# The convolution's taps of two recurrences, moved from VectorE, ScalarE and GpSimd to TensorE

## The chip, the cores and the metric

The kernel runs on one core of a Trainium2 chip. The metric is the device time of one launch in microseconds (us); lower is better. The core has a matrix engine (TensorE, in the profile PE, with its weight loads apart as PEld), a vector engine (VectorE, DVE), a scalar engine (ScalarE, ACT), a general engine (GpSimd, POOL) and a queue that issues transfers (SyncE, SP). Each engine executes its own instruction list in order and waits for others by semaphores.

## The reference

Two layers work on two token streams, `x` and `ctx` (256 tokens of 1024 features each). In each layer a token's 1024 modulated features go through `w_in`; the first 1024 columns of the product feed a convolution path and the rest a linear recurrence (RWKV) of 8 heads. The two halves, 512 features each, are joined and multiplied by `w_out`; then comes a gated feed-forward block.

The convolution path is what the change touches:

```
def conformer_conv(u, conv_w, conv_b, cnorm_g, cnorm_b):
    val, gate = jnp.split(u, 2, axis=-1)
    z = val * jax.nn.sigmoid(gate)
    z = dwconv(z, conv_w) + conv_b          # 31 taps along the 256 tokens, one filter per channel
    z = group_norm(z, CONV_GROUPS, cnorm_g, cnorm_b, LN_EPS)   # 8 groups of 64 channels
    return jax.nn.silu(z)
```

The depthwise convolution has 31 taps, 512 channels and 256 tokens. The scale and shift of every norm ("modulation") come from a vector `c` times `ada_w` (1024 x 6144 per layer), cut into six parts.

## The kernel before

Activations are kept with features on the partitions: a 512-feature tensor is four tiles of 128 x 256 ("four features" below). Weights arrive as 512 KB tiles of 128 x 1024 fp32 through `raw` (L345 to L349), which has four slots in turn. A large weight is split into a high and a low part, `wh` (ScalarE, L341) and `wl` (VectorE, L342; a few on GpSimd, L365), and multiplied as three fast products (`mm3`). The modulation weights are not split: `ada_steps` (L478) multiplies each tile with a 32-column vector in two fp32 products of 512 columns, and after eight tiles the sum goes through ScalarE (tile `T2b`), four small products with `sel` and a VectorE addition.

A recurrence (`rwkv`, L766) works in chunks: products of the input projection (`w_in`), the inverse of small triangular matrices by some hundred dependent VectorE steps (L953 to L969) with 32x32 and 64x64 products, `reads` (L1035), `values` (L1052 to L1071), and then a `chain` of four steps for each of two head groups (L1083 to L1133). Four recurrences are in the program. The first (stream `ctx`, layer 0, about 100 to 260 us) and the last (stream `x`, layer 1, about 1100 to 1350 us) run in the mode "wide": both groups side by side, and with a filler. The filler is a generator of other work, of which the loop over the chain draws six steps (`fill(FILL)`) after each of its eight chain steps: first the convolution's input projection (`conv_in`, four steps), then the modulation vectors (`ada_steps`, 16 steps). After the recurrence of these two the convolution `conv` is emitted whole.

The order in the code is not the order of an engine. A scheduler takes all instructions, with the emitted order as priority, and gives each engine a fixed list by its own estimate of when operands and buffers are ready. So taps emitted after the recurrence are placed into gaps of VectorE, ScalarE and GpSimd during it.

The taps before: of the 30 taps beside the middle one, VectorE takes 13 (first recurrence) or 14 (last) as multiply-add in place (L726), ScalarE 3 or 4 as a product (L730), GpSimd 14 or 12 as a product (L732); GpSimd adds those of ScalarE and its own (L733). The tile `tap` has two buffers, shared by ScalarE and GpSimd. VectorE joins the two sums and the bias at L737. Then comes the group norm (L745): a mean product with a constant, a subtraction on VectorE, a square on ScalarE, a sum product, a reciprocal square root, and four products that spread it. A third convolution, of `z` in layer 0, is done by GpSimd alone, five taps at a time in the background of a feed-forward block and a recurrence. In PSUM the filler's lane has the tag `pb` (two buffers) to itself while the recurrence has the others.

Of the kernel before, what the change touches and what calls it, by code (L numbers as in the profile page):

```python
# [11 lines left out]
AF = mybir.ActivationFunctionType  # L12
ALU = mybir.AluOpType

P = 128
D = 1024
NF = 8
T = 256
# [6 lines left out]
LN_EPS = 1e-5  # L25
# [12 lines left out]
NPOOL, NPOOLE, NPOOLC = (14, 3), (12, 4), (30, 0)  # L38
NTAP = 2

# [127 lines left out]
def _layout(a):  # L168
    f = {}
    n = {k: np.asarray(v) for k, v in a.items()}  # L170
# [38 lines left out]
    for l in range(2):  # L209
        f[f"ada{l}"] = n["ada_w"][l].reshape(4, 2, P, 12, 512).transpose(3, 0, 2, 1, 4).reshape(48, P, 1024)  # L210
        w = n["w_in"][l]
# [7 lines left out]
        f[f"wo{l}"] = (n["w_out"][l].reshape(NF, P, D))  # L219
        lo = np.zeros((P, 2, 1024), np.float32)  # L220
# [15 lines left out]
        w = n["w_in_2"][l]  # L236
# [22 lines left out]
class Prog:  # L259
# [441 lines left out]
    def conv(self, l, z, acc, npool, hold=False):  # L701


        nc = self.nc
        o = COLS[f"convw{l}"][0]
        taps = sorted((j for j in range(31) if j != 15), key=lambda j: abs(j - 15))
        nv, na = 30 - npool[0] - npool[1], npool[1]
        parts = [("v", taps[:nv]), ("a", taps[nv : nv + na]), ("p", taps[nv + na :])]

        order = []  # L710
        for k, js in parts:
            order += [((i + 0.5) / len(js), k, j) for i, j in enumerate(js)]
        order.sort()
        zc = [acc[:, f, :] for f in range(4)]
        for f in range(4):
            w = lambda j: self.cols[:, o + 4 * j + f : o + 4 * j + f + 1]
            av = self.T1([P, T]) if nv else None
            if nv:
                nc.vector.tensor_scalar(av, z[:, f, :], w(15), None, ALU.mult)
                nc.gpsimd.memset(zc[f], 0.0)  # L720
            else:
                nc.gpsimd.tensor_scalar(zc[f], z[:, f, :], w(15), None, ALU.mult)
            for i, (_, k, j) in enumerate(order):
                d, s = slice(max(0, 15 - j), min(T, T + 15 - j)), slice(max(0, j - 15), min(T, T + j - 15))
                if k == "v":
                    nc.vector.scalar_tensor_tensor(av[:, d], z[:, f, s], w(j), av[:, d], ALU.mult, ALU.add)  # L726
                else:
                    t = self.t(self.pool, [P, T], "tap", bufs=NTAP)
                    if k == "a":
                        nc.scalar.mul(t[:, d], z[:, f, s], w(j))  # L730
                    else:
                        nc.gpsimd.tensor_scalar(t[:, d], z[:, f, s], w(j), None, ALU.mult)  # L732
                    nc.gpsimd.tensor_add(zc[f][:, d], zc[f][:, d], t[:, d])  # L733
                if i % 5 == 4:
                    yield
            if nv:
                nc.vector.scalar_tensor_tensor(zc[f], av, self.col(f"convb{l}", f), zc[f], ALU.add, ALU.add)  # L737
            else:
                nc.gpsimd.tensor_scalar(zc[f], zc[f], self.col(f"convb{l}", f), None, ALU.add)
            yield  # L740
        while hold and not self.go:
            yield
        self.group_norm(zc, f"cng{l}", f"cnb{l}", LN_EPS, AF.Silu)
# [668 lines left out]
    def first(self):  # L1412
        nc = self.nc
# [4 lines left out]
        alone = {"r": ("ps", "acc00", "acc01"), "t": ("acc10", "acc11"), "b": ("pb",), "c": ("acc11",), "cs": ("acc10",)}  # L1418
# [6 lines left out]
        def wide(l, x, s0, ada, perm, before=None):  # L1425

            def filler():

                steps = itertools.chain(self.conv_in(l, x, fl(self.x[0])), self.ada_steps(l, ada))
# [14 lines left out]
            self.on("c")  # L1444
            drain(self.conv(l, fl(self.x[0]), fl(self.x[1]), (NPOOL, NPOOLE)[l]))
# [37 lines left out]
        self.bg = self.conv(0, zx, acc, NPOOLC, True)  # L1483
# [155 lines left out]
```

## Time and profile before

| what | us |
|---|---|
| time, median of 3 runs (lowest, highest) | 2779.92 (2776.57, 2785.88) |
| the profiled execution's own time | 2783.58 |
| its span, first to last instruction | 2781.8 |
| busy in the span: PE | 2632.1 (95%) |
| busy: PEld | 2291.3 (82%) |
| busy: DVE | 1716.4 (62%) |
| busy: ACT | 1327.3 (48%) |
| busy: POOL | 670.2 (24%) |

The profile is of one execution. Busy time is the time in which an engine had an instruction in work, and a busy TensorE can be at either of two clocks, so its share has to be read with the granted clock beside it (1.00 is 2.4 GHz, 0.50 is 1.2 GHz). A matmul in fp32 leaves two records in the trace, so a row "x4" of fp32 products may be two products. Idle time is put down to the engine or transfer that ended it.

### The profile page before, as it was taken

What the parts mean: (1) busy time and instruction counts of PE and PEld (TensorE: products, weight loads), DVE (VectorE), ACT (ScalarE), POOL (GpSimd) and SP (SyncE); (2) the same over time, 40 slices, a digit from 0 to 9 for tenths busy, and PEclk for the clock granted to TensorE, in tenths of its full rate; (3) what the DMA queues carried; (4) which work ended last, traced back from release to release, by engine and by line L of the source; (5) the groups of instructions that cost most, each with busy time, mean ns of one, the idle gap of its engine ahead of it and who ended that gap; (6) DMA issues with size and microseconds to landing.
All of it is one profiled execution on the core that took longest, in us unless ns stands there. A gap on an engine that the chain in (4) does not pass through costs nothing.

```text
span 2781.8 us, 53780 instructions
## 1 busy us (share of the span) xinstructions
PE 2632.1 (95%) x22398; PEld 2291.3 (82%) x22398; DVE 1716.4 (62%) x2703; ACT 1327.3 (48%) x2015; POOL 670.2 (24%) x669
## 2 busy tenths in 40 slices
PE   7889989999889998899899899999999999999998
PEld 4866867888678896866699899889899898889897
DVE  3885778645577555984555655666655655755655
ACT  5523654434565346433544544654544544644543
POOL 0388999920130001384200000010000000100000
PEclk9989989999899999979899999999999999999999
DMA  7345425334323354234355555524555555425653
GB/s 250 109 145 175 147 84 180 132 130 157 117 77 116 136 182 144 95 137 153 117 187 185 194 183 188 193 87 156 182 187 185 182 188 174 166 83 182 205 184 120
DMA packets 118768, 430.71 MB, mean 155 GB/s; under 512 B 13174, under 2 KB 13686, under 8 KB 118524
## 3 DMA queue, kind: packets, MB, share of 16 engines
q1 hardware_dynamic: 118524, 427.28, 45.2%
q8 instruction: 175, 2.87, 0.4%
q14 instruction: 69, 0.57, 0.1%
HBM read 425.13 MB, written 2.10 MB: 154 GB/s over the span
## 4 chain that ended last, share of the span: by engine, by line
PE 78%; DVE 11%; ACT 4%; POOL 3%; issue 2%; DMA 2%; SPq 0%; ACTq 0%; DVEq 0%; POOLq 0%
PE pb L333 33%; PE acc L333 25%; PE ps L333 19%; DVE wl L342 3%; DVE T1c L726 1%; POOL tap L732 1%; DVE S L964 1%; DVE T L962 1%; DMA raw<-in_ada 1%; DVE x L621 1%; ACT wh L341 1%; POOL x L733 1%; PE acc L438 1%; DMA raw<-in_wr 0%; DVE T2b L620 0%
## 5 line engine op out<-in xcount | busy, mean ns | idle before, releaser
L342 DVE TENSOR_TENSOR wl<-raw,wh 128x1024 fp32r<-128x1024 f32 (+1 forms) x654 | 811.9, 1245 | 622.2 <-ACT wh L341 391.7
L341 ACT CAST wh<-raw 128x1024 fp32r<-128x1024 f32 (+1 forms) x654 | 681.9, 1046 | 892.3 <-PE pb L333 345.8
L333 PE MATMUL pb<-xf,wh 128*128 128x256 f32 (+1 forms) x2560 | 486.4, 289 | 12.6 <-ACT T1b L585 4.1
L333 PE MATMUL pb<-S,wh 128*128 128x256 f32 x2560 | 492.0, 289 | 4.8 <-DVE S L631 1.8
L333 PEld LDWEIGHTS pb<-xf,wh 128*128 128x128 f32 (+1 forms) x2560 | 409.8, 194 | 26.7 <-DVE T1b L588 6.6
L333 PEld LDWEIGHTS pb<-S,wh 128*128 128x128 f32 x2560 | 408.5, 192 | 22.4 <-issue 11.8
L333 PE MATMUL ps<-S,wh 128*128 128x256 f32 x2048 | 390.4, 287 | 0.6 <-ACT S L460 0.5
L333 PE MATMUL pb<-xf,wl 128*128 128x256 f32 (+1 forms) x1280 | 371.2, 291 | 8.7 <-DVE wl L342 8.7
L365 POOL TENSOR_TENSOR wl<-raw,wh 128x1024 fp32r<-128x1024 f32 x22 | 54.9, 2504 | 1340.4 <-ACT wh L364 826.9
L333 PE MATMUL pb<-S,wl 128*128 128x256 f32 x1280 | 367.4, 287 | 2.0 <-DVE wl L342 2.0
L333 PEld LDWEIGHTS ps<-S,wh 128*128 128x128 f32 x2048 | 326.8, 192 | 9.0 <-issue 3.4
L333 PE MATMUL ps<-S,wl 128*128 128x256 f32 x1024 | 293.4, 286 | 0.6 <-DVE wl L342 0.6
L333 PEld LDWEIGHTS pb<-xf,wl 128*128 128x128 f32 (+1 forms) x1280 | 248.1, 194 | 16.7 <-DVE wl L342 11.5
L333 PEld LDWEIGHTS pb<-S,wl 128*128 128x128 f32 x1280 | 245.4, 192 | 6.6 <-issue 3.0
L333 PE MATMUL acc<-wh,T 128*128 128x512 f32 x704 | 206.3, 393 | 0.0
L333 PEld LDWEIGHTS ps<-S,wl 128*128 128x128 f32 x1024 | 196.7, 192 | 2.8 <-issue 1.4
L333 PE MATMUL acc<-wh,T1b 128*128 128x512 f32 x528 | 157.5, 396 | 3.5 <-ACT T1b L341 3.5
L732 POOL TENSOR_SCALAR tap<-z,cols 128x255 f32<-128x255 f32 (+14 forms) x120 | 149.2, 1252 | 0.0
L333 PEld LDWEIGHTS acc<-wh,T 128*128 128x128 f32 x704 | 126.9, 189 | 23.6
L732 POOL TENSOR_SCALAR tap<-x,cols 128x246 f32<-128x246 f32 (+6 forms) x104 | 111.4, 1079 | 46.1 <-DVE x L671 46.0
L733 POOL TENSOR_TENSOR x<-x,tap 128x247 f32<-128x247 f32 (+8 forms) x132 | 106.8, 809 | 34.4 <-ACT tap L730 28.0
L733 POOL TENSOR_TENSOR z<-z,tap 128x255 f32<-128x255 f32 (+14 forms) x120 | 112.8, 940 | 3.9
(445 smaller groups left out, 3968.7 us busy)
## 6 DMA issues: line engine op xcount, KB each, us to landing
raw<-in_fu SPq DMA_DIRECT2D x132, 512.0 KB, 3.2
raw<-in_ada SPq DMA_DIRECT2D x96, 512.0 KB, 4.3
raw<-in_pu SPq DMA_DIRECT2D x88, 512.0 KB, 4.2
raw<-in_qu SPq DMA_DIRECT2D x88, 512.0 KB, 3.7
raw<-in_fd SPq DMA_DIRECT2D x66, 512.0 KB, 3.2
raw<-in_wr SPq DMA_DIRECT2D x51, 512.0 KB, 3.6
raw<-in_pd SPq DMA_DIRECT2D x44, 512.0 KB, 4.1
raw<-in_qd SPq DMA_DIRECT2D x44, 512.0 KB, 3.8
```

What stands on the lines that cost most here:

```text
L333: return self.nc.tensor.matmul(out, lhsT, rhs, start=start, stop=stop, **kw)
L341: self.nc.scalar.copy(hi, src)
L342: self.nc.vector.tensor_sub(lo, src, hi.bitcast(F32))
L365: self.nc.gpsimd.tensor_sub(lo, r, hi.bitcast(F32))
L438: nc.tensor.transpose(pt[f // 2][:, f % 2, b, :], yb[b][:, f * P : f * P + P], self.cst("ident"))
L621: nc.vector.tensor_add(x[b][:, s], x[b][:, s], t)
L726: nc.vector.scalar_tensor_tensor(av[:, d], z[:, f, s], w(j), av[:, d], ALU.mult, ALU.add)
L732: nc.gpsimd.tensor_scalar(t[:, d], z[:, f, s], w(j), None, ALU.mult)
L733: nc.gpsimd.tensor_add(zc[f][:, d], zc[f][:, d], t[:, d])
L962: nc.vector.tensor_mul(tv, tj[:, k + 1 : 32, k : k + 1].broadcast_to([P, m, k + 1]), X[:, k : k + 1, 0 : k + 1].broadcast_to([P, m, k + 1]))
L964: nc.vector.tensor_sub(X[:, k + 1 : 32, 0 : k + 1], X[:, k + 1 : 32, 0 : k + 1], tv)
```

## The change

In the first and in the last recurrence the taps become TensorE products. For each of the four features the 31 taps are 31 fp32 products of a 128x128 diagonal matrix (the filter's weights of one tap on the diagonal) with a shifted slice of `z`, summed in one PSUM tile; ScalarE adds the bias on the way out. The diagonals are loaded from a new input `cd`, 16 tiles of 512 KB per layer with eight taps each, through the same four `raw` slots. The new generator `conv_pe` and its group norm are steps of the filler, between `conv_in` and `ada_steps`. The third convolution keeps its GpSimd form; `conv` loses the code for the other engines.

```diff
+TAPS = sorted(range(31), key=lambda j: abs(j - 15))
...
+        cw = n["conv_w"][l].reshape(31, 4, P)
+        cd = np.zeros((4, 4, P, 8, P), np.float32)
+        for i, j in enumerate(TAPS):
+            for f_ in range(4):
+                cd[f_, i // 8, np.arange(P), i % 8, np.arange(P)] = cw[j, f_]
+        f[f"cd{l}"] = cd.reshape(16, P, D)
...
+    def conv_pe(self, l, z, acc):
+
+        for f in range(4):
+            pc = self.ps((P, T))
+            for i, j in enumerate(TAPS):
+                if i % 8 == 0:
+                    r = self.raw(f"cd{l}", f * 4 + i // 8)
+                d, s = slice(max(0, 15 - j), min(T, T + 15 - j)), slice(max(0, j - 15), min(T, T + j - 15))
+                self.mm(pc[:, d], r[:, i % 8 * P : i % 8 * P + P], z[:, f, s], i == 0, i == 30)
+                if i % 8 == 7:
+                    yield
+            self.nc.scalar.activation(acc[:, f, :], pc, AF.Identity, bias=self.col(f"convb{l}", f))
+            yield
+        self.group_norm([acc[:, f, :] for f in range(4)], f"cng{l}", f"cnb{l}", LN_EPS, AF.Silu)
+        yield
...
-        alone = {"r": ("ps", "acc00", "acc01"), "t": ("acc10", "acc11"), "b": ("pb",), "c": ("acc11",), "cs": ("acc10",)}
+        alone = {"r": ("ps", "acc00", "acc01"), "t": ("acc10", "acc11"), "b": ("pb",), "cs": ("pb",)}
...
-                steps = itertools.chain(self.conv_in(l, x, fl(self.x[0])), self.ada_steps(l, ada))
+                steps = itertools.chain(self.conv_in(l, x, fl(self.x[0])), self.conv_pe(l, fl(self.x[0]), fl(self.x[1])),
+                                        self.ada_steps(l, ada))
...
-            self.on("c")
-            drain(self.conv(l, fl(self.x[0]), fl(self.x[1]), (NPOOL, NPOOLE)[l]))
```

In the rows below, `raw` with `csil` is a modulation product, `raw` with `x_67` a tap (`x_67` is the convolution's input of that recurrence, `x_68` its result), `acc` and `ps` are PSUM tiles of the recurrence and `pb` one of the filler. First PE's list in the first recurrence before, after the last product of `conv_in` and one modulation half:

```order
L1035 MATMUL acc_239_1489<-const,S_496 128x128 x4
L333 MATMUL pb_2215<-raw_2216,csil 32x512 x2
L1035 MATMUL acc_240_1495<-const,S_496 128x128 x4
L333 MATMUL pb_2215<-raw_2220,csil 32x512 x2
L1052 MATMUL acc_244_1504<-const,S_299 64x128 x4
L333 MATMUL pb_2215<-raw_2224,csil 32x512 x2
L333 MATMUL acc_245_1511<-S_885,S_493 64x64 x4
L333 MATMUL acc_246_1512<-S_885,S_493 64x64 x4
L333 MATMUL pb_2215<-raw_2228,csil 32x512 x2
```

The 32 modulation tiles of this recurrence stand in this way between its rows. After the change, where `conv_in` ends and the first such tiles stood, PE's list reads:

```order
L341 MATMUL pb_2105<-xf_242,wl_2102 128x256
L341 MATMUL pb_2157<-x_67,raw_2158 128x256
L341 MATMUL pb_2157<-x_67,raw_2158 128x255 x2
L341 MATMUL acc_236_1468<-S_1098,S_496 64x64 x2
L341 MATMUL acc_237_1469<-S_1098,S_496 64x64 x2
```

The taps have taken the places of the modulation tiles. Those have moved behind the chain; PE's list after, towards the end of the same recurrence:

```order
L341 MATMUL pb_2635<-raw_2644,csil 32x512 x2
L341 MATMUL pb_2635<-raw_2648,csil 32x512 x2
L341 MATMUL pb_2654<-const,T2b_2652 128x2 x4
L341 MATMUL pb_2660<-raw_2661,csil 32x512 x2
L341 MATMUL pb_2660<-raw_2665,csil 32x512 x2
L341 MATMUL pb_2660<-raw_2723,csil 32x512 x2
L341 MATMUL pb_2660<-raw_2727,csil 32x512 x2
L341 MATMUL pb_2733<-const,T2b_2731 128x2 x4
```

Nothing of the recurrence stands between these rows any more. The group norm's products of the convolution (`x_68`, `T1b`) now stand among the chain's, in PE's list after:

```order
L341 MATMUL ps_2834<-S_956,st_2572 64x64 x3
L341 MATMUL pb_2490<-T1b_2487,const 128x256
L341 MATMUL pb_2494<-T1b_2487,const 128x256
L341 MATMUL acc_446_2810<-T_445_2808,S_1785 64x64
L341 MATMUL acc_447_2811<-T_445_2808,S_1785 64x64
```

A product of the norm that has to wait holds up the chain's products behind it. On POOL the list after goes from the recurrence's set-up to the third convolution:

```order
L470 TENSOR_TENSOR S_2952<-T1b_2993,S_2950 128x256
L939 TENSOR_TENSOR S_1867<-S_1867,T_501_3043 128x256
L939 TENSOR_TENSOR S_1867<-S_1867,T_504_3055 128x256
L732 TENSOR_SCALAR z_5712<-z_3103,cols 128x256
L736 TENSOR_SCALAR tap_5747<-z_3103,cols 128x255
```

Before, the 124 instructions of the recurrence's own taps (on `x_67` and `x_68`) stood ahead of the `z` rows.

## Rows read from the trace of the kernel before

**Rows 1.** the page's chain that ended last, by engine and by line

```profile
PE 78%; DVE 11%; ACT 4%; POOL 3%; issue 2%; DMA 2%; SPq 0%; ACTq 0%; DVEq 0%; POOLq 0%
PE pb L333 33%; PE acc L333 25%; PE ps L333 19%; DVE wl L342 3%; DVE T1c L726 1%; POOL tap L732 1%; DVE S L964 1%; DVE T L962 1%; DMA raw<-in_ada 1%; DVE x L621 1%; ACT wh L341 1%; POOL x L733 1%; PE acc L438 1%; DMA raw<-in_wr 0%; DVE T2b L620 0%
```

**Rows 2.** windows: length, busy us (instructions) by engine, PEclk, DMA share, GB/s

```profile
163.42:258.05 94.63, 94.10 (x1262) 61.83 (x1262) 60.31 (x131) 33.58 (x62) 71.15 (x82) 0.82 0.53 183
1199.35:1350.00 150.65, 145.92 (x1559) 101.01 (x1560) 93.68 (x200) 53.06 (x93) 81.55 (x97) 0.84 0.40 141
130.00:163.42 33.42, 25.99 (x333) 22.42 (x331) 33.42 (x60) 9.12 (x16) 31.07 (x30) 1.00 0.35 117
1150.00:1199.35 49.35, 40.61 (x495) 35.87 (x495) 48.11 (x94) 17.37 (x28) 30.77 (x31) 0.98 0.34 118
```

**Rows 3.** waits of PE in 130 to 163 us: us in total, times, longest

```profile
PE pb L333 <- DVE wl L342: 3.8, 3, 1.9
PE acc L333 <- DVE S L1029: 2.7, 2, 2.4
```

**Rows 4.** windows, VectorE's taps (L726) alone

```profile
131.00:189.00 58.00, 24.48 (x39) 0.91 0.50 170
1168.00:1224.00 56.00, 24.86 (x42) 0.94 0.51 179
```

**Rows 5.** windows of 10 us in both wide recurrences

```profile
190.00:200.00 10.00, 10.00 (x174) 7.46 (x169) 5.30 (x9) 5.88 (x9) 9.68 (x12) 0.70 0.26 92
...
200.00:210.00 10.00, 10.00 (x151) 8.69 (x149) 3.44 (x8) 3.33 (x6) 6.89 (x10) 0.50 0.01 4
...
230.00:240.00 10.00, 10.00 (x156) 6.79 (x153) 3.49 (x10) 2.18 (x5) 7.35 (x10) 1.00 0.76 278
...
1245.00:1255.00 10.00, 10.00 (x124) 7.74 (x125) 3.51 (x7) 2.17 (x4) 9.52 (x13) 0.50 0.01 2
```

**Rows 6.** timeline of PE: start, duration, instruction, count, idle time before it

```profile
56.51 1.02 PE L333 MATMUL ps<-wa,S 128*128 128x256 f32 x4
57.37 2.05 PE L333 MATMUL acc<-S,T 128*128 128x512 f32 x4
```

**Rows 7.** timeline, PE weight loads of 128x128 fp32

```profile
30.29 0.97 PEld L333 LDWEIGHTS ps<-const,T 128*128 128x128 f32 x8
```

**Rows 8.** timeline, PE, products with split weights

```profile
48.18 0.40 PE L333 MATMUL ps<-xf,wh 128*128 128x256 f32 x2
48.42 0.28 PE L333 MATMUL ps<-xf,wl 128*128 128x256 f32 x1
48.54 0.40 PE L333 MATMUL acc<-xf,wh 128*128 128x256 f32 x2
```

**Rows 9.** timeline, PE, modulation tiles with nothing else beside them

```profile
23.20 1.05 PE L333 MATMUL acc<-raw,csil 128*32 128x512 f32 x4
...
28.92 1.05 PE L333 MATMUL pb<-raw,csil 128*32 128x512 f32 x4 [0.21 <-DMA raw<-in_ada]
```

**Rows 10.** windows, the same modulation stage

```profile
20.00:30.00 10.00, 7.80 (x37) 1.93 (x34) 0.56 (x3) 1.63 (x3) 0.00 (x0) 1.00 0.91 318
```

**Rows 11.** timeline, ACT and PE, at the end of the last recurrence's chain

```profile
1270.32 0.50 ACT L730 ACTIVATE tap<-x,cols 128x247 f32<-128x247 f32 x1 [3.59 <-POOL x L733]
...
1270.85 0.38 ACT L1102 ACTIVATE xf<-acc 64x256 f32<-64x256 f32 x1
...
1271.28 0.69 PE L333 MATMUL acc<-xf,S 128*64 128x64 f32 x16 [1.56 <-ACT xf L1102]
...
1277.11 0.26 PE L333 MATMUL ps<-zer 1*128 1x256 bf16 x1 [1.40 <-ACT S L1131]
```

**Rows 12.** timeline, POOL and PE, in the second recurrence

```profile
390.49 2.58 POOL L365 TENSOR_TENSOR wl<-raw,wh 128x1024 fp32r<-128x1024 f32 x1
...
400.00 0.74 PE L333 MATMUL ps<-S,S 64*32 64x32 f32 x28 [4.16 <-DVE S L850]
```

**Rows 13.** windows, the same place

```profile
390.00:400.00 10.00, 2.98 (x14) 2.42 (x12) 5.47 (x7) 6.99 (x12) 10.00 (x7) 0.59 0.33 107
```

More of the change, by code (lines that the diff above doesn't have):

```diff
@@ L36 @@
 NLAST = 2, 4
-NPOOL, NPOOLE, NPOOLC = (14, 3), (12, 4), (30, 0)
 NTAP = 2
+TAPS = sorted(range(31), key=lambda j: abs(j - 15))
 QB, QE, QC, EVERY = (2, 3, 4, 5), (2, 3, 4, 5), (1,), 2
@@ L699, in mixed_in, with conv @@
         return mix
-    def conv(self, l, z, acc, npool, hold=False):
+    def conv_pe(self, l, z, acc):
[12 more added lines that the diff above has]
+        yield
+    def conv(self, l, z, acc):
         nc = self.nc
         o = COLS[f"convw{l}"][0]
[L706 to L713, printed above, removed]
         zc = [acc[:, f, :] for f in range(4)]
@@ L716, in conv @@
             w = lambda j: self.cols[:, o + 4 * j + f : o + 4 * j + f + 1]
[L717 to L723, printed above, removed]
-                d, s = slice(max(0, 15 - j), min(T, T + 15 - j)), slice(max(0, j - 15), min(T, T + j - 15))
[L725 to L733, printed above, removed]
+            nc.gpsimd.tensor_scalar(zc[f], z[:, f, :], w(15), None, ALU.mult)
+            for i, j in enumerate(TAPS[1:]):
+                d, s = slice(max(0, 15 - j), min(T, T + 15 - j)), slice(max(0, j - 15), min(T, T + j - 15))
+                t = self.t(self.pool, [P, T], "tap", bufs=NTAP)
+                nc.gpsimd.tensor_scalar(t[:, d], z[:, f, s], w(j), None, ALU.mult)
+                nc.gpsimd.tensor_add(zc[f][:, d], zc[f][:, d], t[:, d])
                 if i % 5 == 4:
                     yield
[L736 to L739, printed above, removed]
+            nc.gpsimd.tensor_scalar(zc[f], zc[f], self.col(f"convb{l}", f), None, ALU.add)
             yield
-        while hold and not self.go:
+        while not self.go:
             yield
@@ L1482, in first @@
         self.go = False
-        self.bg = self.conv(0, zx, acc, NPOOLC, True)
+        self.bg = self.conv(0, zx, acc)
         self.mods, self.every = self.ada_steps(1, QC), EVERY
```

## The prediction

> **What bounds the kernel now.** I read the chain of waits first: 78% of it is PE, in products of all kinds, 11% VectorE, and of the taps only 1% on VectorE and 2% on GpSimd [rows 1]. So what a change does to TensorE's own work is what counts, and elsewhere only where PE stands still. Next I read the two wide recurrences in windows [rows 2]. Each has two parts. In the first part (130 to 163 us, 1150 to 1199 us) VectorE is full (33.42 of 33.42 us, 48.11 of 49.35) and PE has gaps: 7.4 us (33.42 - 25.99) and 8.7 us (49.35 - 40.61). The waits name VectorE as what ends the gaps, by its weight splits and the evacuations L1029 [rows 3], and of VectorE's time there and just after it the taps take 24.5 and 24.9 us [rows 4]. In the second part (163 to 258, 1199 to 1350 us) PE is busy for 94.10 of 94.63 us and 145.92 of 150.65 us, but at a mean granted clock of 0.82 and 0.84 [rows 2]. In 10 us slices the clock stands at full speed (1.00, 2.4 GHz) while modulation tiles stream in (DMA share 0.76 at 230 us), and at half speed (0.50, 1.2 GHz) where only small products run and hardly a byte arrives (DMA share 0.01 at 200 and at 1245 us) [rows 5]. So half speed is where the recurrence has TensorE to itself, with many short products of 64 columns.
>
> **What is added to TensorE.** 31 taps for four features are 124 fp32 products in a recurrence, 248 in all, of a 128x128 diagonal with at most 256 columns. The nearest row is a product of the same type, stationary size and columns: four records, two products, begin at 56.51 and the next row begins at 57.37, so a product takes 0.43 us [rows 6]. Taps off the middle are shorter: by 2 x (1 + ... + 15) = 240 columns in a feature, so the mean is 256 - 240/31 = 248.3 columns, 0.417 us. 124 x 0.417 = 51.7 us, and twice that is **+103.4 us** on the engine that ends the chain. The order of the changed kernel has them in PE's list between the recurrence's products, in the places where the modulation products stood; those are not removed, they come later.
>
> Here the Trainium skill speaks against the change more strongly than the row. "TensorE: Matmul & The Clock Gate", Part 3 ("The mechanism"), says that a weight load runs beside a product in flight only where the two use different row groups of the array; a 128-row diagonal after another 128-row diagonal uses the same. By that rule every load would stand by itself. The two products of [rows 6] also have full 128-row stationaries that differ, and they follow at 0.43 us; the trace does not agree here, and I take the row.
>
> **What is given back.** (1) The gaps of PE in the first parts: with some 25 us of VectorE's work gone from each, VectorE is ahead, and what is late next is PE, which has the taps to fill the gaps with. 7.4 + 8.7 = **-16.1 us**. (2) Gaps of the second parts, 0.5 and 4.7 us, partly behind ScalarE and its taps (a tap at 1270.32 to 1270.82 stands just ahead of the copy that PE waits 1.56 us for [rows 11]): **-4 us**. (3) The clock. If full speed were held through both second parts, PE's busy time would shrink by 94.10 x 0.18 = 16.9 and 145.92 x 0.16 = 23.3 us, 40.2 in all; that is one end. The other is nothing, since the modulation tiles that kept the clock up at 230 us leave their place, and in the last recurrence the changed list still has a stretch of some 300 small products without one tap. I take 60%, **-24 us**, nearer to the full end because the taps stand in most of the stretches that ran at half speed and are dense products, like those of the slices at 1.00.
>
> **What is lost in other places.** (4) The modulation products. Their 32 tiles stood between the recurrence's rows, hidden behind its products; now most of them follow one another at the end, with y's norm alone between them, and behind them 16 transposes of the next input. Where nothing stood beside them, at the start of the kernel, four tiles took 28.92 - 23.20 = 5.72 us, with PE waiting for the transfer [rows 9] and a DMA share of 0.91 [rows 10]: 1.43 us a tile, against 1.05 of PE's work. 32 x (1.43 - 1.05) = 12.2 us in a recurrence, 24.3 us in both, is one end, nothing the other. Four slots are loaded ahead and a part of the tiles still stands beside the chain, but a half also ends in a chain of ScalarE, PE and VectorE (`T2b`), so I take **+10 us**, the lower side of the middle. The 32 new transfers of 512 KB cost nothing as long as they hide behind taps: a tile feeds 8 x 0.417 = 3.3 us of products and arrives alone in 1.43 us. (5) The group norm. It was outside the chain; now its 12 products wait in PE's list among the chain's products, each for VectorE or ScalarE, and what waits behind one is the chain itself, which VectorE and ScalarE in turn wait for. The chain's own waits of that kind are 1.56 and 1.40 us [rows 11]. Twelve of them, in two recurrences half hidden, would be 12 x 1.4 = 16.8 us; the other end is nothing, where the operands are ready before PE gets there. I take **+8 us**. (6) GpSimd. Without some 250 tap instructions it reaches the third convolution sooner, and so the weight splits that wait in its list: one began at 390.49 us, PE stood still for 4.16 us until 400.00 [rows 12] and was busy for 2.98 of the 10 us there [rows 13]. I take **-6 us**, between 0 and the 7.0 us of that gap. ScalarE loses 28 taps and gains 8 evacuations, beside TensorE: nothing.
>
> **The sum.** 103.4 - 16.1 - 4 - 24 + 10 + 8 - 6 = +71.3 us. On the profiled execution's 2783.58 that is 2854.9; the median of the runs is 3.7 below that execution, so **2851 us**, 2.6% slower.
>
> **Rivals.**
> A. *All that can be given back is given back*: the clock in full (-40.2), all gaps (-16.1 and -5.2), GpSimd (-7), no new wait: 103.4 - 68.5 = +35, 2815 us. For it: the taps are the kind of dense work at which the clock stood at 1.00. Against it: the stretch without taps has nothing to raise its clock, and the norm's products are in the chain's way in the list.
> B. *The end of the recurrence binds*: modulation tiles at the speed of their transfers (+24.3), the norm in full (+16.8), and the clock gives back a third (-13): 103.4 - 16.1 - 4 - 13 + 24.3 + 16.8 - 6 = +105, 2885 us. For it: the tiles stand one behind the other in the list, with nothing of the recurrence between them.
> C. *Weight loads are not hidden.* 248 products are 496 records, each with its load of 0.121 us (0.97 us for eight [rows 7]): +60 us on the sum, 2911 us. This is what the page's rule would give. Against it stands the 0.43 us of [rows 6].
> D. *Faster: a tap takes one pass.* If a diagonal product ran like those of the split weights, three of 256 columns in 0.36 us (48.18 to 48.54 [rows 8]), 0.12 us each, the taps would cost 248 x 0.12 = 30 us, less than the 56 us that the gaps and the clock have room for (16.1 and 40.2), and would fit into them: 30 - 16.1 - 4 - 40.2 + 10 + 8 - 6 = -18, 2762 us. It decides from a tap of 0.19 us downward, where 248 taps cost the 48 us that the other terms then give. Against it: the split tiles are cast to another type first and `cd` is not, and the modulation tiles, fp32 straight from `raw` as well, run at fp32 speed.
> E. *The change doesn't do what it says*: the list has all 124 taps in each recurrence and none on VectorE, so this has no share.
>
> **How the numbers follow.** Forecast 0.74 (own range 2821 to 2881: half the distance between the ends is 20 us for the clock, 12 for the modulation tiles, 8 for the norm and 6 for gaps and GpSimd, as independent ones together 26, and 4 more for the price of a product), A 0.10, B 0.09, C 0.03, D 0.04. A change below 0.3% (about 8 us) can't be told from none. D has half its chance below that bound and half within it, and all other cases are slower: faster 0.02, within 0.02, slower 0.96. The range of 8 in 10 takes the forecast's own and A's: 2813 to 2883 us.
>
> **What would show it.** A run of taps in the timeline at 0.43 us a product bears out the sum's first term; 0.12 would be D, 0.67 (0.43 and two loads of 0.121) C. PE's gaps between 130 and 163 us and the VectorE waits in them should be gone. The granted clock of the small products should be above 0.9 in the first recurrence, and still show a slice at half speed in the last one. Behind the chain, modulation tiles should be spaced by 1.0 to 1.4 us, and waits of PE for a transfer of `in_ada` should appear. Waits for `T1b` or `x_68` inside the chain bear out (5). The forecast is wrong if the two recurrences together grow by less than 35 or by more than 105 us.

## The result and the profile after

The changed kernel takes 2879.57 us (median of 4 runs, 2875.63 to 2883.16), the kernel before beside it 2782.90 us (4 runs). The ratio is 1.0348, 95% interval 1.0328 to 1.0368: 3.5% slower. Forecast were 2851 us, slower, and a range of 2813 to 2883 us. So the sign and the range held, and the size was short by some 25 us: +97 us against +71.

The page of the changed kernel, the chain that ended last, by engine and by line (compare [rows 1]):

```profile
PE 83%; DVE 8%; ACT 4%; DMA 3%; issue 1%; POOL 1%; SPq 0%; ACTq 0%; DVEq 0%; POOLq 0%
PE pb L341 38%; PE acc L341 25%; PE ps L341 19%; DVE wl L350 2%; DMA raw<-in_ada 2%; DVE x L629 1%; ACT wh L349 1%; PE acc L446 0%; DVE S L965 0%; ACT L392 0%; DMA raw<-in_wr 0%; DVE S L852 0%; DVE T L963 0%; DVE T2b L628 0%; POOL tap L736 0%
```

The taps of VectorE and GpSimd have left the chain, PE's share rose from 78% to 83%, and loads of `in_ada` went from 1% to 2%. Next the changed kernel in stretches, as windows (us, busy us and instructions by engine, PEclk, DMA share, GB/s): the first parts, the half-speed stretches and the ends of the two recurrences.

```profile
134.00:163.00 29.00, 29.00 (x319) 27.24 (x320) 22.95 (x57) 7.52 (x12) 0.00 (x0) 1.00 0.32 110
1200.00:1240.00 40.00, 40.00 (x489) 37.55 (x487) 36.70 (x92) 13.53 (x21) 0.00 (x0) 1.00 0.36 120
170.00:200.00 30.00, 30.00 (x387) 24.70 (x384) 10.29 (x19) 10.73 (x16) 1.90 (x2) 0.72 0.11 37
1250.00:1290.00 40.00, 38.95 (x501) 33.08 (x496) 13.44 (x26) 12.62 (x20) 1.90 (x2) 0.57 0.09 28
260.00:330.00 70.00, 59.19 (x417) 28.53 (x414) 23.09 (x52) 22.16 (x43) 1.61 (x2) 0.87 0.76 270
1350.00:1420.00 70.00, 61.50 (x371) 26.93 (x369) 20.42 (x53) 16.75 (x32) 7.70 (x12) 0.83 0.64 226
```

In the first parts PE has no gap left (29.00 of 29.00, 40.00 of 40.00; before 7.4 and 8.7 us [rows 2]). The half-speed stretches are still there. New are the ends: PE stands still for 10.8 and 8.5 us in 70, and its clock is not full there either. In the kernel before the stretches behind the chain read:

```profile
258.00:337.60 79.60, 77.80 (x574) 66.64 (x570) 55.35 (x88) 45.90 (x70) 77.00 (x78) 1.00 0.39 127
1300.00:1336.10 36.10, 34.42 (x143) 21.19 (x140) 18.87 (x41) 15.38 (x27) 7.66 (x10) 0.86 0.04 12
```

To see where the 97 us are, I cut each profile at five marks that all kernels have: the first load of `wc`, the first `T1b` from `pb` of the feed-forward block, the first subtraction in the third convolution's norm, the last load of `wr`, the first load of `pu`. The second mark (421 us in the kernel before) lies inside the second recurrence, so the stage "first rec." holds the beginning of that one too. Stage lengths, in us over the kernel before:

| kernel | start | first rec. | second | third | last rec. | rest |
|---|---|---|---|---|---|---|
| before (length) | 92.4 | 328.9 | 324.3 | 378.6 | 418.4 | 1239.2 |
| changed | +4.0 | +52.3 | -6.5 | -4.0 | +48.6 | +1.1 |
| changed, again | +0.4 | +54.3 | -6.5 | -3.9 | +48.4 | +0.9 |
| changed, middle tap alone | +2.6 | +0.2 | +0.3 | -1.3 | +1.0 | -1.6 |
| before, middle tap alone | +2.8 | -7.1 | -3.1 | +0.8 | -10.8 | +4.6 |
| changed in the first alone | +2.2 | +52.5 | -6.6 | -4.1 | +13.6 | -1.6 |
| changed in the last alone | +5.5 | -3.9 | -0.4 | +0.2 | +37.2 | -2.3 |
| changed, bank counter kept | +2.9 | +53.0 | -1.3 | +5.4 | +43.7 | +5.2 |

And what the clock took: over windows of 10 us, the sum of PE's busy time x (1 - granted clock), called "loss" below, from the first load of `wc` to the first of `wo`, and from the last load of `wr` to the last of `wo`. It is read from one profile each; the changed kernel's two profiles give 47.2 and 49.5 us. It measures where the clock was low; it is not time one to one, as a run below shows.

| kernel | loss, first | loss, last | together | PE idle, together |
|---|---|---|---|---|
| before | 21.1 | 23.9 | 45.0 | 32.9 |
| changed | 20.3 | 26.9 | 47.2 | 30.6 |
| changed, middle tap alone | 27.0 | 40.0 | 67.0 | 21.5 |
| before, middle tap alone | 21.2 | 21.6 | 42.8 | 19.7 |
| before, modulation late | 37.3 | 27.0 | 64.3 | 49.6 |
| changed, modulation first | 17.6 | 28.3 | 45.9 | 18.0 |
| changed, taps and modulation in turn | 17.4 | 20.0 | 37.4 | 20.4 |
| changed, taps among the small products | 20.1 | 9.5 | 29.6 | 23.5 |
| changed, again | 21.6 | 27.9 | 49.5 | 31.5 |
| changed in the first alone | 21.5 | 31.1 | 52.6 | 38.6 |
| changed in the last alone | 17.9 | 19.7 | 37.6 | 27.0 |
| changed, bank counter kept | 27.9 | 19.7 | 47.6 | 28.9 |

The loss did not fall from 45 to 21, as the forecast had it; it stayed.

### The profile page after: what moved, and what is told of

It is laid out like the page before. It is cut to its first block, busy times and chain, and to the rows that moved or that the text cites. A ratio compares the mean times of both kernels' runs of the same rounds, so it can differ in the third digit from the quotient of the medians.

```text
span 2877.3 us, 54424 instructions
## 1 busy us (share of the span) xinstructions
PE 2731.5 (95%) x22894; PEld 2376.7 (83%) x22894; DVE 1635.5 (57%) x2579; ACT 1311.4 (46%) x1990; POOL 450.9 (16%) x425
## 3 DMA queue, kind: packets, MB, share of 16 engines
q1 hardware_dynamic: 123132, 444.06, 44.6%
## 4 chain that ended last, share of the span: by engine, by line
PE 83%; DVE 8%; ACT 4%; DMA 3%; issue 1%; POOL 1%; SPq 0%; ACTq 0%; DVEq 0%; POOLq 0%
PE pb L341 38%; PE acc L341 25%; PE ps L341 19%; DVE wl L350 2%; DMA raw<-in_ada 2%; DVE x L629 1%; ACT wh L349 1%; PE acc L446 0%; DVE S L965 0%; ACT L392 0%; DMA raw<-in_wr 0%; DVE S L852 0%; DVE T L963 0%; DVE T2b L628 0%; POOL tap L736 0%
## 5 line engine op out<-in xcount | busy, mean ns | idle before, releaser
L341 PEld LDWEIGHTS ps<-S,wh 128*128 128x128 f32 x2048 | 327.5, 192 | 10.8 <-issue 4.2
L736 POOL TENSOR_SCALAR tap<-z,cols 128x255 f32<-128x255 f32 (+14 forms) x120 | 143.3, 1203 | 0.0
L341 PE MATMUL pb<-x,raw 128*128 128x254 f32 (+15 forms) x496 | 115.7, 389 | 0.0
L341 PE MATMUL acc<-wl,T 128*128 128x512 f32 x352 | 113.1, 395 | 0.0
```

Of the source, the lines that this page charges most:

```text
L341: return self.nc.tensor.matmul(out, lhsT, rhs, start=start, stop=stop, **kw)
```

## The experiments

Theory: a tap costs TensorE its full 0.42 us, wherever it stands; what the other engines' taps had cost before comes back, but the new order spends as much. Rivals: the order alone makes the difference; the weight loads do; the clock was to come back and something stopped it.

**The changed kernel with the middle tap alone.**

```diff
-            for i, j in enumerate(TAPS):
+            for i, j in enumerate(TAPS[:1]):
...
+            for _ in range(3):      # as many filler steps as with all taps
+                yield
```

> The changed kernel with the middle tap alone: 240 of the 248 tap products are left out (and 24 of 32 loads of diagonals). Theory 1 (0.417 us a tap, nothing hidden): 240 x 0.417 = 100 us less than the changed kernel, 2780 us. Theory 2 (each tap also waits for its weight loads, 0.67 us): 160 us less, 2720 us. Theory 3 (a part of the taps stands in gaps or speeds up the clock): clearly less than 100 us are saved, about 2800 us or more.

Measured: 2779.31 us, ratio 0.9989 (0.9969 to 1.0009). Against the changed kernel's 1.0348 that is 0.0359 x 2783 = 99.9 us for 240 taps, 0.416 us each, the number of Theory 1; the 160 us of Theory 2, with weight loads that stand by themselves, are out. In the timeline of the changed kernel's PE (start, duration, instruction, count):

```profile
203.96 4.31 PE L341 MATMUL pb<-x,raw 128*128 128x248 f32 x20
208.20 0.84 PE L341 MATMUL acc<-S,S 64*64 64x64 f32 x16
```

20 records, ten taps, follow at (208.20 - 203.96) / 10 = 0.424 us a tap, as [rows 6] gave it.

That the net agrees to the microsecond is luck in part. The group of the taps in PE's list of groups, in the changed kernel and in this one (count, busy us, mean ns):

```profile
L341 PE MATMUL pb<-x,raw 128*128 128x254 f32 (+15 forms) x496 | 115.7, 389 | 0.0
L341 PE MATMUL pb<-x,raw 128*128 128x256 f32 x16 | 4.9, 399 | 0.1
```

The 240 taps kept PE busy for 115.7 - 4.9 = 110.8 us. By the table above they also took 19.8 us off the loss, and PE's idle time rose by 9.1 us: 110.8 - 19.8 + 9.1 = 100.1. So the mechanism of Theory 3, taps that bring the clock back, is there as well, and its number is not.

**The kernel before with the middle tap alone.**

```diff
         order.sort()
+        if not hold:
+            order = []
```

> The kernel before with the middle tap alone in the two recurrences: the other taps on VectorE, ScalarE and GpSimd are left out. Theory 1 (VectorE's taps cost TensorE the gaps at the start of both recurrences, GpSimd's a gap later): 16 to 23 us less than before, 2760 to 2767 us. Theory 2 (taps beside TensorE are all hidden, and the gaps are filled by other waits): 2780 us. Theory 3 (they cost their 25 us on VectorE in each recurrence): 2733 us.

Measured: 2768.34 us, ratio 0.9929 (0.9903 to 0.9954), so the taps cost 20 us before (13 to 27), Theory 1. In the profile of that kernel the first parts read, as windows:

```profile
125.00:165.00 40.00, 38.78 (x496) 32.75 (x496) 32.96 (x85) 13.57 (x23) 0.00 (x0) 0.99 0.53 188
1140.00:1190.00 50.00, 46.56 (x649) 40.28 (x651) 44.68 (x112) 18.56 (x31) 0.00 (x0) 1.00 0.43 147
```

PE's gaps are 1.2 and 3.4 us there. The two kernels without taps should now be alike, but the one in the changed order takes 0.0060 x 2783 = 17 us more: that is the price of the order, with an uncertainty of some 9 us. And the loss is 67.0 us in it against 42.8 us. So in the new order the recurrences lose 24 us to half speed that they did not lose before, and the taps bring 20 of them back (67.0 to 47.2).

**The kernel before, modulation products held back.** The changed kernel moves the modulation tiles behind the chain; here the move is made alone.

```diff
-steps = itertools.chain(self.conv_in(...), self.ada_steps(l, ada))
+steps = itertools.chain(self.conv_in(...), iter([None] * 26), late(self.ada_steps(l, ada)))
# late: each step issues after the chain's third step (issue_after)
```

> The kernel before, taps and all, but with most of the modulation products (about 22 of 32 tiles in each recurrence) held back until the third step of the chain, so that nothing but small products is left in the middle of the recurrence. Theory 1 (the modulation products were what kept the clock up before, and the changed kernel moved them away, so that its taps had to make up for that first): loss to half speed in the two recurrences rises from 45 to about 65 us and the time by 11 to 17 us, 2795 to 2801 us. Theory 2 (the place of the modulation products does not matter for the clock): loss 45 us, 2780 to 2787 us.

Measured: 2820.21 us, ratio 1.0132 (1.0094 to 1.0169), +37 us. The loss came out as Theory 1 had it (64.3 us), the time not: PE's idle time rose too, by 17 us (49.6 against 32.9), which I had not expected. Loss and idle time together rose by 36 us, the two recurrences in the same profile by 22 us only (261.2 + 217.5 against 245.2 + 211.9), so the loss counts more than the time that it costs; the rest of the difference lies in other stages. In the first recurrence's middle that kernel's windows read:

```profile
190.00:200.00 10.00, 10.00 (x156) 8.50 (x157) 2.74 (x6) 3.23 (x6) 9.60 (x13) 0.50 0.01 2
200.00:210.00 10.00, 9.27 (x177) 8.29 (x174) 9.62 (x19) 1.90 (x5) 9.76 (x12) 0.50 0.01 2
210.00:220.00 10.00, 10.00 (x195) 9.37 (x197) 3.79 (x9) 2.82 (x7) 9.68 (x13) 0.72 0.01 3
220.00:230.00 10.00, 5.48 (x131) 4.44 (x129) 4.03 (x9) 1.99 (x5) 9.60 (x13) 0.96 0.01 2
230.00:240.00 10.00, 9.95 (x133) 7.13 (x133) 4.52 (x13) 1.39 (x4) 9.60 (x13) 0.53 0.01 2
240.00:250.00 10.00, 9.11 (x139) 5.61 (x136) 2.65 (x7) 2.43 (x5) 9.68 (x13) 1.00 0.92 326
```

The slices from 180 to 210 us are at 0.50 and the one at 230 us at 0.53; in the kernel before, with tiles there, the slice at 190 us read 0.70 and the one at 230 us 1.00 [rows 5]. Where the held tiles arrive (240 us, DMA share 0.92) the clock is full. So in this list the modulation tiles did keep the clock up, and to move them has a price. They are not the only thing that does: at 210 and 220 us the clock came back to 0.72 and 0.96 with no tile in the slice (DMA share 0.01).

**The order of the changed kernel turned round.** The modulation steps before the taps; and the two in turn.

```diff
-self.conv_in(...), self.conv_pe(...), self.ada_steps(l, ada)
+self.conv_in(...), self.ada_steps(l, ada), self.conv_pe(...)          # first kernel
+self.conv_in(...), mixed(self.ada_steps(l, ada), self.conv_pe(...))   # second: one step of each
```

> The changed kernel with two filler parts swapped: the modulation products come before the taps, so that they stand among the recurrence's rows again, and the taps follow in one dense block at the end. The work is the same. Theory 1 (the taps are plain extra time of TensorE, 0.417 us each, and the gaps that they filled were lost again as waits of the modulation products for transfers and for T2b behind the chain): the waits behind the chain go, about 17 us in both recurrences, 2862 us. Theory 2 (the order also costs the clock): with the modulation products back in their old places the clock rises as well, 2840 to 2850 us. Theory 3 (the order costs nothing): 2880 us.

> The changed kernel with the taps' steps and the modulation steps in turn, so that the list has blocks of either among the recurrence's products up to its end. Theory 1 (the forecast's sum without the clock: taps are plain extra time, and of the order only the waits behind the chain count): as with the modulation products first, 2865 to 2872 us, and the loss to half speed in the two recurrences stays near 47 us. Theory 2 (the mixture holds the clock up): loss below 30 us, about 2852 us.

Measured: 2870.84 us, ratio 1.0318 (1.0280 to 1.0356), and 2871.96 us, 1.0317 (1.0301 to 1.0334). Both are about 8 us below the changed kernel (1.0348, 1.0328 to 1.0368), with intervals that overlap; that is half of Theory 1's 17 us for the first, and too little to be told from none; it is far from Theory 2. The second's time is Theory 1's, but its loss (37.4 us) lies between the two theories. PE's idle time in the recurrences did fall by 12.6 and 10.2 us, but with the taps at the end the loss stays (45.9), and in the second it falls by 10 only.

**Taps among the small products.**

```diff
+                self.fill(4)      # after each reads, and after each ga of values
...
+                self.fill(1)      # after each j of the inverse's second half; conv_pe yields per tap
```

> The changed kernel, with the taps drawn one by one in between the reads, the values and the second half of the inverse, so that in the list they stand singly or by threes among the small products that ran at half speed. The work is the same. Theory 1 (the clock did not come back because no tap stood among the products that run at half speed): with taps there the loss to half speed in the two recurrences, 47 us in the changed kernel, falls below 25 us, and the time by as much, 2850 to 2862 us. Theory 2 (small products run at half speed whatever stands between them): loss 40 us or more, 2870 to 2880 us.

Measured: 2880.15 us (2870.65 to 2888.58), ratio 1.0356 (1.0332 to 1.0380): no gain. But the two recurrences differ. Where the changed kernel's last one had 0.57 over 1250 to 1290, this one's windows read:

```profile
1265.00:1275.00 10.00, 10.00 (x81) 8.84 (x80) 0.76 (x2) 1.55 (x3) 0.00 (x0) 1.00 0.39 133
1275.00:1285.00 10.00, 10.00 (x81) 8.83 (x80) 1.91 (x3) 0.19 (x1) 0.00 (x0) 1.00 0.46 146
1285.00:1295.00 10.00, 10.00 (x161) 8.99 (x160) 1.76 (x4) 2.99 (x6) 0.00 (x0) 0.91 0.20 65
1295.00:1305.00 10.00, 10.00 (x142) 7.82 (x140) 5.97 (x9) 6.38 (x8) 1.90 (x2) 0.58 0.15 54
1305.00:1315.00 10.00, 10.00 (x165) 6.92 (x163) 3.01 (x7) 2.19 (x4) 0.00 (x0) 1.00 0.01 3
```

One slice is near half speed in place of four, the loss there is 9.5 us in place of 26.9, and that stage is 17 us shorter in the same profile (450.0 against 467.0 us; that execution took 2870.65 us, the median is 2880.15). In the first recurrence the loss is 20.1 us, as in the changed kernel: the clock was full from 130 to 190 and from 210 to 250 us, but slices at 0.61 to 0.88 stood between these and slices at 0.52 to 0.88 came at the end, among the chain, the modulation tiles and the transposes. The second stage then took 10 us more than in the changed kernel (328.1 against 317.8). So Theory 1's mechanism is seen in one recurrence, and its gain did not show in the whole.

**One pass.** Taps of the split weights' type.

```diff
+            self.nc.scalar.copy(zr, z[:, f, :])       # z, cast on ScalarE
...
+                    self.nc.scalar.copy(r, rr)        # the diagonals, cast on ScalarE
...
+                self.mm(pc[:, d], r[:, i % 8 * P : i % 8 * P + P], zr[:, s], i == 0, i == 30)
```

> The changed kernel with taps of the type of the split weights (the diagonals and the convolution's input are cast on ScalarE first; shifts are rounded to even ones, which leaves the count and the size of the products). Theory 1 (a tap's price is its product, in passes): 0.12 in place of 0.417 us, 248 x 0.297 = 74 us less than the changed kernel, 2806 us. Theory 2 (the price is the load of the diagonal, which stays): less than 30 us saved, above 2850 us. Theory 3 (36 casts on ScalarE, some 38 us, come into the chain): 2830 us.

Measured: 2801.88 us, ratio 1.0062 (1.0043 to 1.0080), 0.0286 x 2783 = 80 us below the changed kernel; Theory 1 gave 74. PE's timeline in that kernel has 18 taps in 2.35 us:

```profile
154.21 2.35 PE L341 MATMUL pb<-tap,wh 128*128 128x254 f32 x18
```

That is 0.13 us each; all 248 together kept PE busy for 44.6 us in place of 115.7. The price of a tap is its product, not the load of its diagonal. Even so this form is not faster than the kernel before: it is 0.0062 x 2783 = 17 us slower.

**VectorE's taps later, in the kernel before.** PE's gaps came from VectorE being full in the first parts; perhaps the taps need only move.

```diff
+                    with self.tc.issue_after(self.inv_end.ins):
                         nc.vector.scalar_tensor_tensor(av[:, d], z[:, f, s], w(j), av[:, d], ALU.mult, ALU.add)
...
+            self.inv_end = nc.vector.tensor_sub(...)      # each step of the inverse; the last one stays
```

> The kernel before, with one difference: VectorE's taps in the two recurrences are held back until the last step of the triangular inverse (L964), so that they stand beside the second part, where VectorE has room. TensorE has nothing of the taps. Theory 1 (what taps cost before were TensorE's gaps at the start of both recurrences, 16 us, and these come from VectorE being full there): nearly all of what leaving the taps out gave, 2766 to 2772 us. Theory 2 (the taps only move the waits into the chain of the second part): 2780 us or above.

Measured: 2808.14 us, ratio 1.0089 (1.0068 to 1.0110): 25 us slower, on the side of Theory 2 (2780 us or above). The four longest waits of PE in its first recurrence (130 to 260 us; us in total, times, longest):

```profile
PE acc L333 <- ACT xf L1103: 7.0, 1, 7.0
PE acc L333 <- DVE T L1066: 4.4, 2, 3.3
PE acc L1036 <- DVE S L1030: 2.9, 2, 2.5
PE ps L333 <- ACT S L1132: 2.1, 1, 2.1
```

Waits inside values and chain (L1066, L1103, L1132) came in. VectorE had room there on the whole, 60 busy us in 95 [rows 2], but not at the moments that counted. And the gaps of the first part did not go:

```profile
130.00:165.00 35.00, 28.41 (x326) 23.93 (x317) 34.18 (x68) 8.68 (x15) 32.55 (x33) 0.94 0.43 152
```

With nearly all of its taps held back VectorE is still full (34.18 of 35.00 us), and PE has 6.6 us of gaps. GpSimd's taps are still there (32.55 us busy), and beside them VectorE's other steps take longer. One step of the inverse in the first parts, in the kernel before, in this kernel and in the changed one, where GpSimd is idle (0.00 us busy in the windows above):

```profile
L962 DVE TENSOR_TENSOR T<-S,S 128x255 f32<-128x255 f32 x2 | 1.4, 675 | 0.0
L963 DVE TENSOR_TENSOR T<-S,S 128x255 f32<-128x255 f32 x2 | 1.8, 878 | 0.0
L963 DVE TENSOR_TENSOR T<-S,S 128x255 f32<-128x255 f32 x2 | 0.8, 422 | 0.0
```

675 and 878 ns against 422. So a part of what filled VectorE before came from the taps on GpSimd. No run leaves out GpSimd's taps alone, so how the gaps divide between the two engines stays open.

**One recurrence at a time.** In each kernel one recurrence has the taps on TensorE, the other the old `conv` (here `conv_old`).

```diff
-                steps = itertools.chain(self.conv_in(...), self.conv_pe(...), self.ada_steps(l, ada))
+                cv = [self.conv_pe(...)] if l == 0 else []      # or l == 1
+                steps = itertools.chain(self.conv_in(...), *cv, self.ada_steps(l, ada))
...
+            if l == 1:                                          # or l == 0
...
+                drain(self.conv_old(l, fl(self.x[0]), fl(self.x[1]), NPOOLE))
```

> The change in the first recurrence alone; the last keeps the taps of the kernel before. Theory 1 (each recurrence pays for its own 124 taps): half of the 97 us, 2828 to 2834 us, and the granted clock of the first recurrence is about 0.85, as before. Theory 2 (the last recurrence pays more, since its modulation tail or its half-speed stretch is longer): below 2825 us. Theory 3 (the first pays more): above 2837 us.

> The change in the last recurrence alone; the first keeps the taps of the kernel before. Theory 1 (the two recurrences add up, and what the first-only kernel showed beside its first recurrence, 13.6 us more in the untouched last one, was the luck of another list): the first recurrence at 329 us as before, the last stage at 467 us, in all about 49 us over before, 2830 to 2834 us. Theory 2 (the recurrences add up by their times: 97 - 56): 40 us over before, 2822 to 2826 us.

Measured: 2839.72 us, ratio 1.0205 (1.0184 to 1.0225), and 2817.96 us, 1.0134 (1.0083 to 1.0185). The sum of the two, 57 + 37 = 94, fits the 97. The first kernel's total is in the range of its Theory 3 (above 2837 us), but not because the first recurrence pays more. The shares are not even, and the stage table says why: with the first recurrence changed, the last one is 13.6 us longer with its old taps (its loss is 31.1 us in place of 23.9), and with taps on TensorE it is 467.0 us long in place of 455.6. Something reaches from the first recurrence into the last, worth 11 to 14 us. So Theory 1 of the last-alone kernel was wrong on its stage (467 expected, 455.6 measured), and Theory 2's 40 us fits.

**The bank counter.** One thing that could reach that far is the counter that chooses the next PSUM bank: `conv_pe` takes four tiles, and a recurrence has three banks in turn.

```diff
             pc = self.ps((P, T))
+            self.psn -= 1
```

> The changed kernel, where the taps' four PSUM tiles no longer advance the counter that chooses the next PSUM bank of the recurrences (one line). The work is the same; the first recurrence's list stays, and the last recurrence's becomes nearly that of the kernel changed in the last alone (99% of its rows in the same order, against 71% for the changed kernel). Theory 1 (the first recurrence's taps made the last one longer only by this counter, and so by the list): the last stage at 455 to 457 us in place of 467, in all 2866 to 2870 us, the first stage still at 381 to 383. Theory 2 (what comes from the first recurrence into the last is something else): 467 us, 2877 to 2880 us.

Measured: 2891.77 us (2884.16 to 2895.38), ratio 1.0367 (1.0341 to 1.0393), not to be told from the changed kernel. The last stage fell to 462.1 us, not quite half of the way, so neither theory holds, and the loss in it from 26.9 to 19.7, as in the last-alone kernel (19.7). But the second and third stages rose by 14.6 us (from -6.5 and -4.0 to -1.3 and +5.4). The part behind the last recurrence is 5.2 us longer as well, and over all these kernels it moves from -2.3 to +5.2 us, so a part of such a difference can be of one execution. The counter changes the lists of stages far from the change; what that is worth, some 5 us in the last stage, is no more than this spread. Why the last recurrence depends on the first by 11 to 14 us is only half explained and stays open.

**The changed kernel once more.**

> The changed kernel once more with a profile, for how far readings of one profile repeat. If they do: loss to half speed 45 to 49 us in the two recurrences, the stage of the first recurrence 381 us within 2, of the last 467 us within 2, and the 4 us more ahead of the first recurrence again. If that 4 us was of one execution: 92 to 94 us ahead of it.

Measured: one run of 2877.24 us. The stages repeat within 2 us and the loss within 2.3 (49.5); the 4 us ahead of the first recurrence do not (92.8 us).

## Why the prediction was right, and which term was off

**Taps on TensorE, +103.4.** Right in price and short in size: a tap takes 0.424 us in a row of ten, but all 248 kept PE busy for 115.7 us, 12 us more than the term, some of them at half speed. The 0.416 us of the run with one tap is a net, with a part of the clock in it. Rival C (0.67 us a tap) is out by the row of ten, and D's price needs another type, which the taps do not have; with that type D's sum had 18 us less than before, and 17 us more were measured. The rule of the Trainium skill ("TensorE: Matmul & The Clock Gate", Part 3, "The mechanism") that loads overlap only across row groups is not borne out by these rows. The same section of the Trainium skill also lets a load go ahead into a background weight buffer; no run here shows whether that is what happens.

**Gaps of the first parts, -16.1.** Right: they are gone, 0 of 69 us in the windows above. The reason is right in part: VectorE was full there, but with its own taps held back it stayed full beside GpSimd's.

**The clock, -24.** This is the term that failed: the loss went from 45.0 to 47.2 us, and where the text expected more than 0.9 in the first recurrence, 170 to 200 us read 0.72. The step took the taps as dense work that is added where the recurrence ran alone at half speed. In fact they came in exchange: the modulation tiles, whose slice at 230 us stood at 1.00 [rows 5], left the same places. The forecast put that on the far end of its bounds and then chose 60% of the other. The runs show both halves: the order without taps raises the loss to 67.0 us, the taps take it down to 47.2, and moving the modulation tiles alone raises it from 45.0 to 64.3.

A second part lies at the ends, which the forecast took at a full clock. In the two windows of the ends above 59.19 x 0.13 and 61.50 x 0.17 us, together 18.2 of the 47.2, are lost at half speed; in the kernel before it was nothing from 258 us and 34.42 x 0.14 = 4.8 us from 1300 us. So ahead of the ends the loss did fall, from 40.2 to 29.0 us, by some 11 of the 24, and the ends took 13 back. So modulation tiles do not always hold the clock up; this one at the end of the last chain took 1.92 us in place of 1.05:

```profile
1364.26 1.92 PE L341 MATMUL pb<-raw,csil 128*32 128x512 f32 x4 [1.23 <-DMA raw<-in_ada]
```

How much of the ends' loss is time is not shown, since PE also waits for transfers there: the kernel with the bank counter kept lost 27.9 us in its first recurrence in place of 20.3, and that stage was 0.7 us longer.

Where a tap did stand at half speed, it cost more itself, and the small products beside it took nearly twice as long. Taps and the same 32 records before and after the clock rose, in the changed kernel, and the windows around them:

```profile
185.86 1.98 PE L341 MATMUL acc<-xf,T 64*64 64x64 f32 x32
...
189.41 4.95 PE L341 MATMUL pb<-x,raw 128*128 128x242 f32 x14
194.30 0.68 PE L341 MATMUL acc<-S,S 64*64 64x64 f32 x13
...
202.42 1.15 PE L341 MATMUL acc<-xf,T 64*64 64x64 f32 x32
```

```profile
180.00:190.00 10.00, 10.00 (x184) 8.62 (x183) 4.11 (x8) 4.62 (x8) 0.12 (x1) 0.64 0.01 3
...
200.00:210.00 10.00, 10.00 (x127) 8.68 (x123) 1.82 (x5) 1.98 (x4) 0.00 (x0) 1.00 0.31 104
```

The small products took 1.98 us in the slice that reads 0.64 (it holds both clocks) and 1.15 us at 1.00. The seven taps (14 records) from 189.41 us took 4.89 us to the next row, 0.70 us each in place of 0.424. The stretch without taps that the text named was there in both recurrences, not in the last alone.

**Modulation products behind the chain, +10.** Right in kind and short in size. PE's timeline after the chain, in the changed kernel:

```profile
295.12 1.05 PE L341 MATMUL pb<-raw,csil 128*32 128x512 f32 x4
297.09 1.05 PE L341 MATMUL pb<-raw,csil 128*32 128x512 f32 x4 [0.92 <-DMA raw<-in_ada]
298.47 1.05 PE L341 MATMUL pb<-raw,csil 128*32 128x512 f32 x4 [0.33 <-DMA raw<-in_ada]
299.74 1.05 PE L341 MATMUL pb<-raw,csil 128*32 128x512 f32 x4 [0.21 <-DMA raw<-in_ada]
301.53 1.05 PE L341 MATMUL pb<-const,T2b 128*128 128x2 f32 x8 [0.74 <-ACT T2b L505]
```

The spacing is 1.3 to 2.0 us, where 1.0 to 1.4 was forecast, and both waits are there. The two ends have 10.8 + 8.5 = 19.3 us of idle time, twice the term, so what the gaps gave was spent here: PE's idle time in the recurrences is 30.6 us after and 32.9 us before.

**Group norm in the chain, +8.** Wrong: it costs next to nothing in waits. The waits of PE at the end of the first recurrence of the changed kernel, 260 to 330 us:

```profile
PE pb L341 <- ACT T2b L505: 4.4, 6, 0.7
PE pb L341 <- DMA raw<-in_ada: 3.9, 8, 1.0
PE pb L446 <- DVE mod L511: 0.9, 1, 0.9
PE pb L341 <- DVE T1b L393: 0.7, 1, 0.7
PE pb L341 <- ACT T1b L462: 0.6, 1, 0.6
PE pb L446 <- DVE T1b L466: 0.3, 1, 0.3
```

One wait of 0.7 us is the norm's (`T1b`, L393). No other of its products has a wait here, so their operands were ready before PE came to them, the lower end of the bounds.

**GpSimd, -6.** The stages after the first recurrence are 10.5 us shorter, but not for that reason: the wait it was meant to end has grown, and nearly all of it lies ahead of the mark (421 us before, 478 us after) behind which the 10.5 us are counted. In the second recurrence PE waited for `S` (L850) 6.7 us in all before (365 to 445 us), and in the changed kernel (420 to 500 us, L851):

```profile
PE ps L341 <- DVE S L851: 10.3, 4, 5.5
```

Kernels with other lists and GpSimd just as free have there -1.0 us (middle tap alone), -6.6 (one pass) and +4.1 (bank counter kept). So the 10.5 us belong to one list more than to the change.

Together: the two recurrence stages grew by 52.3 + 48.6 = 100.9 us, under the 105 above which the forecast called itself wrong, and 25 us were missing in all (97 against 71). The clock term was off by 26, the norm by -8, the ends by some 9 and the stages after the first recurrence by -4, which makes 23. The gaps and the ends paid for each other, and the clock term is the one that decides the size. The close fit of that sum is luck in part: with the 115.7 us that the taps were busy in place of 103.4 it would be 12 us more, and what gave some 10 us back beside them no run here shows. The sign rests on the price of the taps, which the runs show; that the time came inside the range rests also on errors that cancel.

## What to carry to other kernels

Work moved onto the engine that ends the chain costs its price, less the time in which that engine really waits and that it fills; count such time first (here 16 us for 103 us of work). Before work is put into a place, look at what it pushes out of it, and where that goes: what filled the place may have been doing the same service, here in part for TensorE's clock. A full engine may be full because of its neighbour: look at how long its own steps take with and without the neighbour's work. In a scheduled kernel a difference of 5 to 15 us in a stage that the change doesn't touch can be another list, so price a term by leaving the work out in both orders, and not by one stage.

## What was not expected of the hardware

A stretch of small products at half speed takes up to twice as long and looks fully busy (10.00 of 10 us at 0.50 [rows 5]; 1.98 us for records that take 1.15 at 1.00), so neither the busy share nor the waits show it; only the granted clock does.

What brings the clock back is not one kind of work. In the kernel with the modulation products held back it was full in the slice in which they arrived (240 us), but also near full twenty us earlier with no tile there (0.96 at 220 us); and in the changed kernel a modulation tile at the end of a chain took 1.92 us in place of 1.05. Why the clock falls and rises where it does stays open.

VectorE's steps take longer while GpSimd works: the same step of 128x255 took 675 ns in the kernel before, with GpSimd busy for 31.07 of 33.42 us [rows 2], and 422 ns in the changed kernel, with GpSimd idle.

And the clock's readings are not alike in all profiles: in the one-pass kernel long even stretches (1400 to 1550 us) read 0.95 where others read 1.00, so its loss was not compared.
